# Interleaving two arrays on one core: 32 KiB store rows on two queues against 64 KiB store rows on one

## The chip, the cores and the metric

The kernel runs on one core of a Trainium2 chip. The metric is the device time of one execution in microseconds (us), given as the median of several runs. The work uses the core's 16 DMA engines, which move data between HBM (the chip's memory) and SBUF (the core's on-chip memory of 128 partitions), and VectorE (DVE), which copies within SBUF. SyncE (SP) and ScalarE (ACT) only issue DMAs here; each has a DMA queue of its own, and both queues feed the same 16 engines.

## The reference

Two float32 arrays of shape 32 x 256 x 1024 (8,388,608 elements, 33.5 MB each) are interleaved element by element into one of 32 x 256 x 2048 (67.1 MB):

```
result = np.zeros((batch, seq, dim * 2), dtype=np.float32)
result[..., 0::2] = x
result[..., 1::2] = y
```

Nothing is computed on the numbers. Since the interleave doesn't care where a row of 1024 ends, the arrays can be treated as flat: element i of x goes to 2i, element i of y to 2i + 1.

## The kernel before

The flat arrays are cut into 8 tiles of 128 partitions x 8192 elements (`WL`), 4 MiB of x and 4 MiB of y each. In a tile, partition p holds a contiguous run of 32 KiB of each input, and its output is a contiguous run of 64 KiB.

The loop over tiles (L44) loads x (L58) and y (L59) of a tile with one DMA each, on SP's queue; each moves one row of 32 KiB per partition. For the first tile, x is loaded in two halves, one on SP's queue and one on ACT's (L52 to L56). The pools `xpool` and `ypool` have two buffers each, so loads run up to two tiles ahead. After the first tile's loads, the "early" DMA (L64 to L67) writes 16 rows of 512 B from the y tile into the output region of the last tile, on ACT's queue, once y has landed. These bytes are overwritten by the last tile's own store; the write has no part in the result.

An inner loop (L70) takes the tile in two halves of 4096 columns (`WS`). For each half, DVE copies x into the even columns of an output buffer (L80) and y into the odd columns (L81), and ACT issues the store (L82): 128 rows of 32 KiB, each half of an output run. `opool` has two such output buffers of 32 KiB per partition. In SBUF the buffers take 64 + 64 + 64 = 192 KiB per partition.

The order of instructions on each engine is chosen by a scheduler from the program and its buffer dependencies; waits on semaphores are put in where a buffer is read or reused. Each transfer ends with one small packet per DMA engine that counts up the semaphore of that transfer.

After compiling, `tile_interleave_kernel` moves the first DMA of SP and of ACT ahead of the opening barrier (L97 to L115) and shortens the end (L120 to L129): GpSimd waits for the last transfers and clears the semaphores. The change does not touch this.

Of the kernel before, what the change touches and what calls it, by code (L numbers as in the profile page):

```python
# [3 lines left out]

# [4 lines left out]


@with_exitstack
def _interleave(
    ctx: ExitStack,
    tc: tile.TileContext,
    x: bass.AP,
    y: bass.AP,
    out: bass.AP,
):
    nc = tc.nc  # L20
    P = 128

    total = 1
    for s in x.shape:
        total *= s

    WL = 8192
    WS = 4096

    xf = x.rearrange("b s d -> (b s d)")  # L30
    yf = y.rearrange("b s d -> (b s d)")
    of = out.rearrange("b s d -> (b s d)")

    fp32 = mybir.dt.float32

    xpool = ctx.enter_context(tc.tile_pool(name="xp", bufs=2))
    ypool = ctx.enter_context(tc.tile_pool(name="yp", bufs=2))
    opool = ctx.enter_context(tc.tile_pool(name="op", bufs=2))

    lwidths = [WL] * (total // P // WL)  # L40
    assert sum(lwidths) == total // P

    start = 0
    for lw in lwidths:  # L44
        xtile = xpool.tile([P, WL], fp32, name="xtile")[:, :lw]
        ytile = ypool.tile([P, WL], fp32, name="ytile")[:, :lw]

        xs = dataclasses.replace(xf, offset=start, ap=[[lw, P], [1, lw]])
        ys = dataclasses.replace(yf, offset=start, ap=[[lw, P], [1, lw]])
        if start == 0:  # L50

            for q, c in ((nc.sync, 0), (nc.scalar, lw // 2)):  # L52
                q.dma_start(
                    out=xtile[:, c : c + lw // 2],
                    in_=dataclasses.replace(xf, offset=c, ap=[[lw, P], [1, lw // 2]]),
                )  # L56
        else:
            nc.sync.dma_start(out=xtile, in_=xs)  # L58
        nc.sync.dma_start(out=ytile, in_=ys)  # L59

        if start == 0:


            early = dataclasses.replace(  # L64
                of, offset=2 * (total - P * WL), ap=[[2 * WL, 16], [1, 128]]
            )
            nc.scalar.dma_start(out=early, in_=ytile[:16, :128])  # L67

        soff = 0
        while soff < lw:  # L70
            width = min(WS, lw - soff)
            otile = opool.tile([P, 2 * WS], fp32, name="otile")[:, : 2 * width]
            os_ = dataclasses.replace(
                of,
                offset=2 * start + 2 * soff,
                ap=[[2 * lw, P], [1, 2 * width]],
            )
            xsub = xtile[:, soff : soff + width]
            ysub = ytile[:, soff : soff + width]
            nc.vector.tensor_copy(out=otile[:, 0::2], in_=xsub)  # L80
            nc.vector.tensor_copy(out=otile[:, 1::2], in_=ysub)  # L81
            nc.scalar.dma_start(out=os_, in_=otile)  # L82
            soff += width

        start += P * lw
    assert start == total


def kernel(tc, x, y, out):
    nc = tc.nc  # L90
    _interleave(tc, x, y, out)
    tc.close()
    tc.compile()  # L93


    blocks = nc.main_func.blocks
    for engine in (mybir.EngineType.SP, mybir.EngineType.Activation):  # L97
        opening = blocks[0].instructions
        at, moved = next(
            (b, i)  # L100
            for b in blocks[1:]
            for i in b.instructions
            if i.engine == engine and i.opcode == "DMACopy"
        )
        assert not moved.sync_info.on_wait
        body = at.instructions
        body.remove(moved)
        gate = next(
            n
            for n, i in enumerate(opening)  # L110
            if i.engine == engine and i.opcode == "Drain"
        )
        opening.insert(gate, moved)
        at.instructions = body
        blocks[0].instructions = opening  # L115

    last = nc.main_func.blocks[-1]  # L120
    tail = last.instructions
    wait = tail[0]
    clear = next(n for n, i in enumerate(tail) if i.opcode == "ISA")
    assert wait.engine == mybir.EngineType.SP and wait.opcode == "Drain"
    assert wait.sync_info.on_wait and not wait.sync_info.on_update
    assert tail[clear].engine == mybir.EngineType.Pool
    last.instructions = [
        copy.replace(wait, engine=mybir.EngineType.Pool)
    ] + tail[clear:]  # L129


# [1 line left out]
_INS = ['x', 'y']  # L133
_OUTS = [((32, 256, 2048), 'float32')]


# [23 lines left out]
```

## Time and profile before

| what | value |
|---|---|
| median of 5 runs | 315.53 us (315.35 to 315.86) |
| the profiled execution | 315.58 us |
| its span, from the first to the last instruction | 313.8 us |
| bytes read from and written to HBM | 67.11 and 67.12 MB |
| mean rate over the span | 428 GB/s |
| DVE busy | 72.6 us (23%), 32 copies |
| L80, x copies 128 x 4096, each | 2295 ns |
| L81, y copies 128 x 4096, each | 2292 ns |
| DMA packets in all | 4784, of these 544 under 512 B |

How to read it: a DMA is cut into packets, one per row, spread evenly over the 16 engines; a packet has a start and a duration in the trace. The page's rows on queues give packets, MB, and the time that the packets took as a share of 16 engines' span. "q1" is SP's queue, "q10" ACT's. In an answer of the windows view, each row gives the stretch, its length, busy time and number of instructions of DVE and POOL, the granted TensorE clock, the DMA share and the GB/s moved. DMA shares above 1 come from counting a packet where it starts.

### The profile page before, as it was taken

To read this page: it belongs to the slowest core of one execution; us is meant where nothing else is said; L and a number is where in the kernel's file an instruction comes from. 1 tells how busy PE (TensorE), PEld (TensorE's weight loads), DVE (VectorE), ACT (ScalarE), POOL (GpSimd) and SP (SyncE) were. 2 spreads that over 40 slices of the span, in tenths; PEclk is the share of its full clock that TensorE was granted. 3 is DMA by queue.
4 is the path that set the end of the run, shared out by engine and by line. 5 is a ranking of instruction groups with operands and counts; after the bars stand their busy time and mean duration, and the time that the engine had idled before them with its cause. 6 is when DMAs were issued, how large, how long until landed. Compare 5 with 4: busy or idle time off the path is not lost.

```text
span 313.8 us, 139 instructions
## 1 busy us (share of the span) xinstructions
DVE 72.6 (23%) x32; POOL 0.2 (0%) x4
## 2 busy tenths in 40 slices
DVE  0523002231022410325003150131501305023500
POOL 0000000000000000000000000000000000000000
DMA  8999999999999999999999999999999999999997
GB/s 343 460 409 394 455 414 455 414 455 414 455 414 451 418 439 430 430 439 418 451 414 455 409 460 405 464 401 468 401 464 405 460 409 455 414 455 414 455 414 334
DMA packets 4784, 134.23 MB, mean 428 GB/s; under 512 B 544, under 2 KB 560, under 8 KB 560
## 3 DMA queue, kind: packets, MB, share of 16 engines
q10 hardware_dynamic: 2480, 69.22, 51.1%
q1 hardware_dynamic: 2304, 65.01, 48.4%
HBM read 67.11 MB, written 67.12 MB: 428 GB/s over the span
## 4 chain that ended last, share of the span: by engine, by line
DMA 83%; DVE 11%; DVEq 1%; issue 0%
DMA out_dram<-otile 76%; DMA ytile<-in_y_dram 7%; DVE otile L81 6%; DVE otile L80 5%; DVEq L93 1%; DVEq L80 0%
## 5 line engine op out<-in xcount | busy, mean ns | idle before, releaser
L80 DVE COPY otile<-xtile 128x4096 f32<-128x4096 f32 x16 | 36.6, 2295 | 185.8 <-DMA out_dram<-otile 174.1
L81 DVE COPY otile<-ytile 128x4096 f32<-128x4096 f32 x16 | 36.6, 2292 | 40.0 <-DMA ytile<-in_y_dram 40.0
L144 POOL MEMSET const-bfloat16-1.0<- 128x1 bf16 x1 | 0.1, 103 | 0.0
L144 POOL MEMSET const-uint8-127<- 128x1 uint8 x1 | 0.1, 103 | 0.0
L144 POOL MEMSET const-float32-1.0<- 128x1 f32 x1 | 0.1, 100 | 0.0
L144 POOL MEMSET const-float32-0.0<- 128x1 f32 x1 | 0.1, 99 | 0.2 <-issue 0.2
## 6 DMA issues: line engine op xcount, KB each, us to landing
out_dram<-otile ACTq DMA_DIRECT2D x16, 4096.0 KB, 29.1
ytile<-in_y_dram SPq DMA_DIRECT2D x8, 4096.0 KB, 60.8
xtile<-in_x_dram SPq DMA_DIRECT2D x7, 4096.0 KB, 43.6
xtile<-in_x_dram SPq DMA_DIRECT2D x1, 2048.0 KB, 11.7
xtile<-in_x_dram ACTq DMA_DIRECT2D x1, 2048.0 KB, 13.4
out_dram<-ytile ACTq DMA_DIRECT2D x1, 8.0 KB, 6.1
```

The costliest lines, as they stand in the source:

```text
L80: nc.vector.tensor_copy(out=otile[:, 0::2], in_=xsub)
L81: nc.vector.tensor_copy(out=otile[:, 1::2], in_=ysub)
L93: tc.compile()
L144: nc = _bacc.Bacc("TRN2", target_bir_lowering=False, num_devices=1)
```

## The change

The tile size stays at 128 x 8192. What changes is how a tile is stored and in which order DMAs are issued:

- the two half-tile output buffers become one buffer of 64 KiB per partition (`opool`, one buffer); a store moves 128 rows of 64 KiB, one per tile
- x and y of a tile share one buffer, `pair`, of 64 KiB per partition (x on the left, y on the right), two of them; SBUF use remains 192 KiB
- a weave is two copies of 8192 columns instead of four of 4096
- the last tile is woven not into the output buffer but into the `pair` buffer that tile 6 has left
- all stores and loads are on SP's queue, but for the second half of the first x, which stays on ACT's
- the order is the program's (`manual_schedule`): load 0, load 1, weave and store 0, load 2, weave and store 1, and so on to load 7, weave and store 6, weave and store 7
- the early small write is gone

```diff
-    WL = 8192
-    WS = 4096
+    W = 8192
+    n = total // (P * W)
+    assert n * P * W == total
...
-    xpool = ctx.enter_context(tc.tile_pool(name="xp", bufs=2))
-    ypool = ctx.enter_context(tc.tile_pool(name="yp", bufs=2))
-    opool = ctx.enter_context(tc.tile_pool(name="op", bufs=2))
+    inpool = ctx.enter_context(tc.tile_pool(name="inp", bufs=2))
+    opool = ctx.enter_context(tc.tile_pool(name="op", bufs=1))
+    ctx.enter_context(tc.manual_schedule())
...
+    def rows(flat, k, width):
+        return dataclasses.replace(
+            flat, offset=k * P * width, ap=[[width, P], [1, width]]
+        )
...
-        if start == 0:
-
-            for q, c in ((nc.sync, 0), (nc.scalar, lw // 2)):
+    def load(k):
+        pair = inpool.tile([P, 2 * W], fp32, name="pair")
+        if k == 0:
+            for q, c in ((nc.sync, 0), (nc.scalar, W // 2)):
                 q.dma_start(
-                    out=xtile[:, c : c + lw // 2],
-                    in_=dataclasses.replace(xf, offset=c, ap=[[lw, P], [1, lw // 2]]),
+                    out=pair[:, c : c + W // 2],
+                    in_=dataclasses.replace(xf, offset=c, ap=[[W, P], [1, W // 2]]),
                 )
         else:
-            nc.sync.dma_start(out=xtile, in_=xs)
-        nc.sync.dma_start(out=ytile, in_=ys)
+            nc.sync.dma_start(out=pair[:, :W], in_=rows(xf, k, W))
+        nc.sync.dma_start(out=pair[:, W:], in_=rows(yf, k, W))
+        return pair
 
-        if start == 0:
-
-
-            early = dataclasses.replace(
-                of, offset=2 * (total - P * WL), ap=[[2 * WL, 16], [1, 128]]
-            )
-            nc.scalar.dma_start(out=early, in_=ytile[:16, :128])
+    def weave(pair, woven):
+        for s in (0, 1):
+            nc.vector.tensor_copy(out=woven[:, s::2], in_=pair[:, s * W : (s + 1) * W])
 
-        soff = 0
-        while soff < lw:
...
-            nc.vector.tensor_copy(out=otile[:, 0::2], in_=xsub)
-            nc.vector.tensor_copy(out=otile[:, 1::2], in_=ysub)
-            nc.scalar.dma_start(out=os_, in_=otile)
-            soff += width
...
+    pairs = {0: load(0)}
+    for k in range(n):
+        if k + 1 < n:
+            pairs[k + 1] = load(k + 1)
+            woven = opool.tile([P, 2 * W], fp32, name="woven")
+        else:
+            woven = inpool.tile([P, 2 * W], fp32, name="pair")
+        weave(pairs.pop(k), woven)
+        nc.sync.dma_start(out=rows(of, k, 2 * W), in_=woven)
```

More of the change, by code (lines that the diff above doesn't have):

```diff
@@ L34, in _interleave @@
     fp32 = mybir.dt.float32
-    xpool = ctx.enter_context(tc.tile_pool(name="xp", bufs=2))
-    ypool = ctx.enter_context(tc.tile_pool(name="yp", bufs=2))
-    opool = ctx.enter_context(tc.tile_pool(name="op", bufs=2))
[L40 to L49, printed above, removed]
-        if start == 0:
-            for q, c in ((nc.sync, 0), (nc.scalar, lw // 2)):
+    inpool = ctx.enter_context(tc.tile_pool(name="inp", bufs=2))
@@ L59, in _interleave @@
-        nc.sync.dma_start(out=ytile, in_=ys)
-        if start == 0:
-            early = dataclasses.replace(
-                of, offset=2 * (total - P * WL), ap=[[2 * WL, 16], [1, 128]]
-            )
-            nc.scalar.dma_start(out=early, in_=ytile[:16, :128])
-        soff = 0
-        while soff < lw:
[L71 to L79, printed above, removed]
-            nc.vector.tensor_copy(out=otile[:, 0::2], in_=xsub)
-            nc.vector.tensor_copy(out=otile[:, 1::2], in_=ysub)
-            nc.scalar.dma_start(out=os_, in_=otile)
-            soff += width
@@ L85, in _interleave @@
-        start += P * lw
-    assert start == total
+                    out=pair[:, c : c + W // 2],
+                    in_=dataclasses.replace(xf, offset=c, ap=[[W, P], [1, W // 2]]),
+                )
+        else:
+            nc.sync.dma_start(out=pair[:, :W], in_=rows(xf, k, W))
[4 more added lines that the diff above has]
+            nc.vector.tensor_copy(out=woven[:, s::2], in_=pair[:, s * W : (s + 1) * W])
```

## The prediction

> **What bounds the kernel now.** I read the page first, then the windows view over the whole span, then the DMA view of two short windows, then the packet records of the trace themselves (start, duration, size and queue of each DMA packet), because the views do not resolve what this change turns on.
>
> ```profile
> span 313.8 us, 139 instructions
> ...
> DVE 72.6 (23%) x32; POOL 0.2 (0%) x4
> ...
> q10 hardware_dynamic: 2480, 69.22, 51.1%
> q1 hardware_dynamic: 2304, 65.01, 48.4%
> ...
> DMA 83%; DVE 11%; DVEq 1%; issue 0%
> ```
>
> Queue 10 is the ACT queue (stores, half of the first x), queue 1 the SP queue (loads). Their packets together fill 51.1 + 48.4 = 99.5% of 16 engines' span. The chain says DMA 83%, DVE 11%, which looks as if 11% could be won from the copies; the queue rows say no: while a copy is on the chain the engines are still moving the other queue's bytes. So the bound is the number of bytes times the pace of an engine, and the only time to win or lose is time in which an engine moves nothing. The windows show where that is:
>
> ```profile
> 0.00:3.10 3.10, 0.00 (x0) 0.20 (x4) 1.00 0.74 233
> 3.10:25.80 22.70, 8.28 (x4) 0.00 (x0) 1.00 1.00 430
> 25.80:29.60 3.80, 0.71 (x1) 0.00 (x0) 1.00 1.14 407
> 29.60:285.00 255.40, 56.83 (x25) 0.00 (x0) 1.00 1.00 433
> ```
>
> The last two columns are the DMA share and GB/s. All is flat at 430 to 433 GB/s but for two places: the first 3 us (233), and 25.8 to 29.6 us (407 although the engines are "1.14" busy: packets that take longer than their bytes need). The second place is where the kernel writes to HBM for the first time. Is one queue alone enough to fill the engines, and is one direction alone as fast as both mixed? Two windows of the DMA view answer, 14 to 25 us (loads only) and 290 to 312 us (stores only):
>
> ```profile
> q1 hardware_dynamic: 164, 4.85, 102.1%
> ```
>
> ```profile
> q10 hardware_dynamic: 320, 9.44, 99.3%
> ```
>
> Yes, in both. Mixing costs nothing either: in the packet records the start-to-start distance on one engine is 1209.3 to 1209.45 ns (means of the four pairs) for a 32 KiB packet from 29.6 us to the end, whichever of load and store it is and whichever comes next.
>
> **The change, step by step, for one of the 16 engines** (the work is split evenly, so one engine's sum is the span's).
>
> 1. *Longer store rows.* Start-to-start distances in the packet records: 23.4 ns for 512 B, 607.06 for 16 KiB, 1209.45 for 32 KiB. From the last two, 16 KiB more cost 602.39 ns, so a packet has 607.06 - 602.39 = 4.7 ns that do not depend on its size; 512 B gives 23.4 - 18.8 = 4.6, the same. A 64 KiB packet is not in the trace; the line through three sizes gives 2 x 1204.78 + 4.7 = 2414.3 ns. Bounds: nothing saved if a row is still moved as two packets (2418.9), 4.7 saved if it is one. A loss is not excluded by a row, but three sizes on one line speak against it. I take one packet: 64 packets less per engine x 4.7 = 0.30 us.
> 2. *Fewer transfers.* Each transfer ends with a 4-byte semaphore packet per engine; the next packet starts 6 ns after it. Before: 17 loads, 16 stores and the early write make 34 (the 544 "under 512 B" of the page are 34 x 16). After: 17 + 8 = 25. 9 x 6 ns = 0.05 us. The early write's data (L67, 8 KB in all) goes too: 23 ns on its engine. Together 0.08 us.
> 3. *All stores on SP's queue.* A store now stands in SP's program behind the wait for its weave, and the next pair's two loads stand behind it. That hurts only if the ring runs dry meanwhile. A pair load of 8 MiB takes 16 x 1209 + 12 ns = 19.4 us, a store 19.3 us. While SP waits for weave k, load k+1 is still running in the ring. One copy of 4096 columns takes 2.29 us and two in a row 4.50 us from start to end, so a weave of two 8192-column copies is 8.8 to 9.1 us. Issues of 0.33 to 0.52 us on SP are hidden the same way.
> 4. *One output buffer.* Weave k+1 must wait until store k has landed. From then: 0.4 us (last store packet to the waiting instruction, 312.81 to 313.21 us) + 9.1 us weave + about 1 us until a fresh issue moves data (0.00 to 0.99 us at the start) = 10.5 us, beside load k+2, 19.4 us long and issued before it. Cover left: 8.9 us per tile, so the cost is nothing; without that cover it would be about 10.5 us for each of 7 tiles.
>    The Trainium skill ("Trainium Kernel Development and Optimization", section Best Practices) says to double-buffer so that DMA and compute overlap, which speaks against this step. By that rule the single buffer would expose the weaves; the rows above say another transfer is in the ring each time.
> 5. *The last tile* goes into the pair buffer that weave 6 has freed. Its weave needs load 7 and weave 6, not store 6, so it runs in the first 9.1 us of store 6 (19.3 us), and store 7 is queued some 10 us before it is needed. The end remains an engine's last packet plus 0.94 us (312.81 to 313.75).
> 6. *Start.* The first x halves, y and the second pair are issued in the same order on the same queues: nothing changes up to 26 us.
> 7. *No early small write.* This is the unknown. Between 25.86 and 27.70 us, 27 load packets take 1.23 to 1.97 us instead of 1213 ns. Their excess sums to 0.73 us per engine. It starts right behind the 512 B packets, and comes back behind the early write's semaphore packets; the first 32 KiB stores at 29.07 us already run at 1213 ns. Two readings: the first write to HBM costs this whoever makes it (then store 0 pays it at about 41 us), or it belongs to the small write and to the switch between queues (then it goes). The nearest row is the other first: the first loads of the kernel take 1088 to 1554 ns for 16 KiB instead of 611, and 0.62 us per engine are lost there. Two firsts, two similar prices: I take "it stays, 0.73". Ends: 0 and, for a first packet of 64 KiB that has nothing to hide behind, twice that (1.46).
>
> **Sum:** 0.30 + 0.08 = 0.385 us less per engine, nothing added. The profiled execution took 315.58 us (span 313.8, 1.8 around it); 315.58 - 0.385 = 315.20. The median of the runs is 0.05 lower (315.53), so the forecast is 315.15 us, 0.12% less than before. About 0.2% (0.63 us) is what a measurement of this kernel can tell from no change (its five runs span 0.16%).
>
> **Rivals.**
> - *The stall of 0.73 us goes with the small write.* For: the loss ends before the first large store, which pays nothing itself. Against: it could be that store's entrance fee, paid early. Then 315.53 - 0.385 - 0.73 = 314.4.
> - *The first write costs more when it is a whole tile's first row*, at most the double: 315.15 + 0.73 = 315.9, still within the bound.
> - *The long row is still two packets*: 0.30 is not saved, 315.45. The change then does nothing that can be seen.
> - *Slower: each turn of the one ring costs.* Before, an engine never goes longer than 3.1 us without a load or without a store packet once stores have begun. After, it loads for 19.4 us, then stores for 19.3, in one ring. After the first write there are 6 more returns to writing and 6 to loading. If a return to writing costs what the first did, 6 x 0.73 = 4.4 us: 319.5. It decides early: the verdict is slower from 0.63 + 0.385 = 1.0 us in all, that is 0.17 us per return to writing, or 0.085 us per turn of either kind. Against it: turns between packets of the two queues, some 3,000 of them, cost nothing; and store-to-store and load-to-load borders within one queue cost 6 ns. What is not in the trace is a turn within a ring, or after a long pause.
>
> The Trainium skill prices a return differently ("HBM Reference", section Latency): 0.2 us on average for an access, 2 us under high load. If 12 turns each cost 0.2 us, the time would be 2.4 us longer; no run here shows such a wait at a turn.
>
> **Chances.** Stall stays: 0.42. Stall gone: 0.32. Stall larger: 0.07. Row still two packets: 0.03. Turns cost: 0.16. So faster by over 0.2% 0.32, within 0.2% 0.52, slower 0.16. The range takes in the gone stall (314.4, and 0.2 for the scatter of runs) and, above, the doubled stall and the mild end of the turns (0.1 us each, 315.15 + 1.2): 314.2 to 316.5. What lies outside is the dear end of the turns. The likeliest case by itself is 314.9 to 315.5.
>
> **What would show it.** In the changed kernel's page: queue 1 near 99% with all but the first half-x, 1024 store packets of 64 KiB and 400 packets under 512 B; DMA digits without a dip. In the packet records: 2414 ns between starts of store packets (step 1); no gap ahead of a store or load (steps 3 to 5), with DVE idle ahead of each weave waiting for the store before; around 41 us load or store packets with an excess, summing to 0.73 us per engine or to none (step 7). The forecast is wrong if packets lengthen at every turn, or if the ring is dry when a store is issued.

## The result and the profile after

The changed kernel takes 317.05 us in the median of 23 runs (315.61 to 318.18); the kernel before, on the same chips, 315.57 us in 44 runs (315.31 to 316.83). The ratio is 1.0037 with an interval of 1.0027 to 1.0047: **slower by 0.4%**, where 0.1% faster was forecast. What stands out is the scatter: 2.6 us between its runs, a few tenths between most runs of the kernel before.

The profiled execution of the changed kernel is its fastest run (315.61 us) and looks like the forecast. Its page:

```profile
span 313.8 us, 88 instructions
...
DVE 70.3 (22%) x16; POOL 0.2 (0%) x4
...
q1 hardware_dynamic: 3456, 132.12, 97.9%
q10 hardware_dynamic: 144, 2.10, 1.6%
...
DMA 71%; DVE 17%; SPq 0%; issue 0%; DVEq 0%
```

One queue carries nearly everything and fills the engines (97.9 + 1.6 = 99.5%, as before with two). 400 small packets and 1024 store packets of 64 KiB are there, and the mean distance from one store packet's start to the next on an engine is 2414.4 ns (forecast 2414.3). The order on SP's and DVE's side is as reckoned, in the timeline (start, duration, engine, line, operation, and idle time ahead with what ended it):

```profile
61.93 8.77 DVE L61 COPY woven<-pair 128x8192 f32<-128x8192 f32 x2 [35.49 <-DMA out_dram<-woven]
70.73 0.34 SPq L71 DMA_DIRECT2D out_dram<-woven  x1
71.17 0.38 SPq L55 DMA_DIRECT2D pair<-in_x_dram  x1
71.59 0.43 SPq L56 DMA_DIRECT2D pair<-in_y_dram  x1
100.63 8.77 DVE L61 COPY woven<-pair 128x8192 f32<-128x8192 f32 x2 [29.93 <-DMA out_dram<-woven]
```

Each weave waits for the store before it (35.49 and 29.93 us of idle DVE) and its own store is issued at 70.73 us, about 8 us before load 2 is through (79 us). The ring, that is what a queue still holds for an engine to move, never runs dry. Windows of the same execution:

```profile
3.10:36.00 32.90, 8.86 (x2) 0.00 (x0) 1.00 1.02 441
36.00:41.20 5.20, 0.00 (x0) 0.00 (x0) 1.00 0.89 315
41.20:60.00 18.80, 0.00 (x0) 0.00 (x0) 1.00 1.03 446
62.00:78.00 16.00, 8.70 (x2) 0.00 (x0) 1.00 1.03 444
```

The stretch from 36 to 41 us, ahead of the first store, is where the loss of the first write now stands (315 GB/s; packets counted where they start make the neighbours look high): 0.85 us per engine, against 0.73 before. So this profile doesn't show why the median is 317.05.

**Where the time is when it takes longer.** The changed kernel was run once more and caught at 318.07 us. The trace doesn't name a packet's engine, but on one engine a packet starts 3 to 4 ns before the last one ends, so packets can be strung into 16 chains. "Excess" below is a packet's duration over 611 ns (16 KiB), 1213 (32 KiB) or 2418 (64 KiB), what such packets take undisturbed. The sum over all engines is no larger than in the 315.61 us execution (1.75 us per engine, 1.79 there). But 15 engines end between 312.0 and 312.9 us and one at 315.4. In the windows view, the end of the execution of 315.61 us, then the end of the repeated one of 318.07 us:

```profile
312.90:315.40 2.50, 0.00 (x0) 0.00 (x0) 1.00 0.00 0
```

```profile
312.90:315.40 2.50, 0.00 (x0) 0.00 (x0) 1.00 0.06 26
```

A share of 0.06 and 26 GB/s is one engine of sixteen at its full pace, alone for 2.5 us. How it came to be late, at the seven changes from loads to stores ("turns"), from the chains:

```
turn at us         39    78.9   117.5   156   195   234   273
late by, us       0.83   0.96    1.86   3.01  3.01  3.10  3.39
its excess, ns     876    474     654    866     0   378     0
others, each  352-1260  0-108    0-56  0-168  0-21  0-16  0-39
```

"Late by" is the start of its last load packet after that of the first engine, "excess" that of its last two load packets ahead of the stores. "Late by" already holds what the last load but one lost: the 866 ns at 156 us are part of the 3.01 us in the same column. At the first turn everybody pays; over the six later ones the late engine loses 2.37 us, each other one 0.01 to 0.17 us, and what it loses it is later by from then on.

### The profile page after: what moved, and what is told of

Same layout as the page of the kernel before. It is cut to its first block, busy times and chain, and to the rows that moved or that the text cites. A ratio compares the mean times of both kernels' runs of the same rounds, so it can differ in the third digit from the quotient of the medians.

```text
span 313.8 us, 88 instructions
## 1 busy us (share of the span) xinstructions
DVE 70.3 (22%) x16; POOL 0.2 (0%) x4
## 3 DMA queue, kind: packets, MB, share of 16 engines
q1 hardware_dynamic: 3456, 132.12, 97.9%
## 4 chain that ended last, share of the span: by engine, by line
DMA 71%; DVE 17%; SPq 0%; issue 0%; DVEq 0%
DMA out_dram<-woven 49%; DMA pair<-in_y_dram 22%; DVE woven L61 15%; DVE pair L61 1%; SPq L55 0%; SPq L71 0%; DVEq L61 0%
## 5 line engine op out<-in xcount | busy, mean ns | idle before, releaser
L61 DVE COPY woven<-pair 128x8192 f32<-128x8192 f32 x14 | 61.4, 4426 | 202.9 <-DMA out_dram<-woven 185.3
L61 DVE COPY pair<-pair 128x8192 f32<-128x8192 f32 x2 | 8.9, 4428 | 5.9 <-DMA pair<-in_y_dram 5.2
```

What stands on the lines that cost most here:

```text
L61: nc.vector.tensor_copy(out=woven[:, s::2], in_=pair[:, s * W : (s + 1) * W])
```

## The experiments

The edits are against the changed kernel unless said otherwise. Each figure is a median with the range of its runs.

**1. The changed kernel again** (no edit).

> The changed kernel again, nothing edited, to see an execution that is slower than the profiled one. The profiled execution took 315.61 us and lost only some 0.2 us per engine in late load packets (1214 to 1221 ns instead of 1213), while the median is 317.05. Theory 'reading alone' (all 16 engines read HBM at once, with no store packets between, and then a read is now and then late): in an execution of 317 us or more the excess of load packets over 1213 ns sums to about 1.5 us per engine, spread over the load stretches; store packets stay at 2418 ns. Rival 'turns': the excess stands in the last load packet ahead of a store or the first packet behind it, some 0.2 us at each of 12 turns. Rival 'first write': it stands at 36 to 41 us, 2.3 us instead of 0.85. Median expected between 316.3 and 317.5 by all three.

Measured: 317.89 us (317.43 to 318.07), the trace above. None of the three expectations describes it. The loss does stand at the turns, but on one engine, not on all. Late loads within the load stretches (1214 to 1221 ns) amount to some 0.1 us per engine, so "reading alone" isn't it; the first write costs 0.75 us, so it isn't that either. From here on I took up "the late reader".

**2. The early small write put back.**

```diff
+        if k == 0:
+            early = dataclasses.replace(
+                of, offset=2 * (total - P * W), ap=[[2 * W, 16], [1, 128]]
+            )
+            nc.scalar.dma_start(out=early, in_=pair[:16, W : W + 128])
```

> The changed kernel with the early small write put back (16 rows of 512 B on ACT's queue when the first y has landed; the last tile's store overwrites it). 'First write': the loss at 36 to 41 us moves to about 26 us and shrinks to 0.73 us per engine, and the median falls to that of the kernel before, about 315.5 us, with a scatter of a few tenths. 'Reading alone' and 'turns': the stall moves, but the median stays at 316.5 to 317.3 us with a scatter of 2 us.

Measured: 317.73 us (316.36 to 318.29). The 512 B packets ran at 26.0 to 26.5 us, and in the windows view nothing happened there:

```profile
24.00:36.00 12.00, 2.51 (x1) 0.00 (x0) 1.00 1.00 429
36.00:41.20 5.20, 0.00 (x0) 0.00 (x0) 1.00 0.91 328
```

The loss stays ahead of the first large store (0.79 us per engine). "First write" as the cause of the median falls. In the same profile the two engines that end last, 2.3 and 1.5 us behind the median engine, lost 2.18 and 1.66 us at the six later turns, the others 0.03 to 0.61 us: the late reader again.

**3. Stores cut into two of 32 KiB rows.**

```diff
-        nc.sync.dma_start(out=rows(of, k, 2 * W), in_=woven)
+        for h in (0, 1):
+            nc.sync.dma_start(
+                out=dataclasses.replace(
+                    of, offset=2 * k * P * W + h * W, ap=[[2 * W, P], [1, W]]
+                ),
+                in_=woven[:, h * W : (h + 1) * W],
+            )
```

> The changed kernel with each store cut in two of 32 KiB rows, as the kernel before stores them (halves of a tile), both on SP's queue; the rest as changed. By the sum of the prediction this costs 64 more data packets x 4.7 ns + 8 semaphore packets x 6 ns = 0.35 us: about 317.4 us. If long rows are themselves the trouble, the median falls to about 315.6 us. 'Reading alone', 'turns' and 'first write' all expect no fall: 317.0 to 317.5 us.

Measured: 318.12 us (317.25 to 318.46), beside 317.89 for the repeat on the same chip. A difference of 0.2 is in line with the 0.35 of the sum, and lies within the scatter. Long rows aren't the trouble. Here too the two engines that end last lost most at the six later turns, 2.98 and 1.98 us, the others 0.03 to 1.17 us.

**4. Tiles of 4096 columns, twice the turns.**

```diff
-    W = 8192
+    W = 4096
```

> The changed kernel with tiles of 4096 columns instead of 8192: 16 tiles, twice as many turns in the ring (28 after the first write instead of 12), each stretch of loads or stores half as long (9.7 us); store rows are 32 KiB. Packets and semaphores cost 0.3 + 0.2 us more by the sum. 'Turns': the 1.5 us that the median lies above the kernel before doubles, 318.5 to 319.5 us. 'Reading alone': the engines read alone for as long in all, so the loss stays, 317.0 to 317.7 us, or falls if a stretch has to last a while before reads get late. 'First write': 317.0 to 317.7 us.

Measured: 323.29 us (322.75 to 324.0). More than "turns" expected: the packets' excess is 5.1 us per engine (1.79 in the 315.61 us execution), it falls on many engines, and the last engine ends 3.4 us behind the median one. From 30 us on, 0.9 us per engine stand in the last four loads ahead of a store, 2.0 in the last store ahead of a load and 0.6 in the first load behind it. The turns are the place, here in both directions; their price is not a constant.

**5. and 6. One engine made late, first try**, in both kernels: 17 rows of the first y loaded again, on ACT's queue.

```diff
+        if k == 0:
+            nc.scalar.dma_start(
+                out=pair[:17, W : W + 512],
+                in_=dataclasses.replace(yf, offset=0, ap=[[W, 17], [1, 512]]),
+            )
```

> The changed kernel, with 17 rows of 2 KiB of the first y loaded a second time on ACT's queue. 17 has no divisor up to 16 but 1, so one engine should get all 17 packets, 17 x 80 ns = 1.4 us more, at about 26 us, and be late from then on; the others get nothing. Theory 'the late reader' (at a turn from loads to stores, the engine that is still on its last loads while the others have begun to write is held up, and is later still at the next turn): this engine pays 0.1 to 0.9 us at most of the six later turns, as the late one did in the repeated run (0.96 us late at the second turn, 3.4 us at the last), and ends 3 to 5 us behind the others: 317.8 to 320 us, and every run is slow, with few near 316. Rival 'a turn costs any engine by chance': the late engine ends 1.4 us late plus what chance gives, 317.5 to 318.5 us, and the excess falls on other engines as often.

> The control: the same 17 extra packets on one engine in the kernel before, whose loads and stores take turns packet by packet out of two queues. The extra load also holds one engine's first pass back by 1.4 us. 'The late reader': there is no stretch in which all others write, so lateness isn't added to; the engine ends 0.9 to 1.4 us after the others and the time is 316.4 to 317.0 us. If lateness costs here too, over 317.5 us.

Measured: 325.17 (324.91 to 325.37) and 320.77 us (319.1 to 321.21). The first tells nothing of the question. The 17 packets took turns with 32 KiB loads of the other queue, one each 1.29 us, and landed at 42 us. The weave of the changed kernel waited for them:

```profile
42.62 4.43 DVE L66 COPY woven<-pair 128x8192 f32<-128x8192 f32 x1 [24.68 <-DMA pair<-in_y_dram]
```

The ring ran dry at 41 us. The extra load has to go where nobody waits for it (experiments 9 and 10). In the kernel before (profile of the 321.21 us run) the rings are dry for only 0.25 us per engine; after 42 us some 210 loads are held up, all along the span, 2.7 us per engine and on every engine. So a kernel on two queues can lose time this way too.

**7. Each store waits until the next pair has landed**, so that no load is left at a turn to stores.

```diff
...
+        if k + 1 < n:
+            nxt = pairs[k + 1]
+            for c in (W - 1, 2 * W - 1):
+                nc.vector.tensor_copy(out=spare, in_=nxt[:, c : c + 1])
+            nc.vector.tensor_copy(
+                out=woven[:, 2 * W - 2 : 2 * W - 1], in_=pair[:, W - 1 : W]
+            )
         nc.sync.dma_start(out=rows(of, k, 2 * W), in_=woven)
```

> The changed kernel, where each store (but the last) is issued only when the next pair has landed: after a weave DVE copies one column of each half of the next pair to a spare column and writes one column of the output again, so nobody reads HBM while others write at a turn from loads to stores. The ring is empty for some 1.7 us at each of 7 such turns (0.4 us landing, 0.3 us of small copies, 1.0 us until an issue moves data): some 12 us more than 315.2, so 326 to 329 us. 'The late reader': no load packet at the later turns is over by more than 30 ns, lateness stays below 1 us, and the runs scatter by a few tenths instead of 2 us. 'A turn costs in itself': the excess stays, now in the first store packets, with the scatter.

Measured: 333.79 us (333.75 to 333.88). Half of the expectation holds: no load packet ahead of a store is held up, and the scatter is gone (0.13 us). But the time is 5 us over. The windows view around two gaps ahead of stores and two returns to loads:

```profile
40.50:42.50 2.00, 0.22 (x2) 0.00 (x0) 1.00 0.00 0
56.00:62.50 6.50, 0.00 (x0) 0.00 (x0) 1.00 0.86 323
82.00:84.10 2.10, 0.22 (x2) 0.00 (x0) 1.00 0.45 187
97.00:104.00 7.00, 0.00 (x0) 0.00 (x0) 1.00 0.80 300
```

The gaps of 1.7 to 2.1 us are as meant. At each of the 6 returns to loads, though, all engines lose 0.82 to 0.88 us, in the last store packet and the first loads, where the changed kernel loses nothing. 315.2 + 7 x 1.9 + 6 x 0.83 = 333.5. The 0.73 us of the first write, which 315.2 holds, is not lost here, while each of the 7 first stores behind a gap loses 0.08 us; with that it is 333.3, half a us short of the measured time. Behind a gap, all 16 engines start within 0.15 us of each other.

**8. The kernel before without its early small write** (the block at L61 to L67 taken out).

> The kernel before without its early small write, nothing else. In the changed kernel with the early write, the 512 B packets at 26 us cost 27 ns each and no load near them was late; the loss stood in the two loads ahead of the first large store. So here the loss should stay at 0.7 us per engine, in the loads ahead of the first store, and the time should be within 0.2 us of the kernel before (315.4 to 315.7). If the small write itself paid, or paid in place of something dearer, the time moves by 0.5 us or more.

Measured: 315.49 us (315.28 to 315.73), ratio 0.9995 (0.9987 to 1.0004). As expected; the loss ahead of the first store is 0.67 us per engine.

**9. One engine made late, with a load that nobody waits for.**

```diff
...
             pairs[k + 1] = load(k + 1)
+            if k == 0:
+                nc.sync.dma_start(
+                    out=spare,
+                    in_=dataclasses.replace(yf, offset=0, ap=[[W, 17], [1, 512]]),
+                )
```

> The changed kernel with 17 rows of 2 KiB of y loaded into a spare tile that nobody reads, on SP's queue behind load 1. All 17 packets go to one engine (the earlier try showed that), 17 x 80 ns = 1.4 us, so one engine comes 0.8 to 1.4 us late to the first turn, and nothing else waits. Theory 'the late reader' (at a turn from loads to stores the engine still loading while others have begun to write is held up): that engine loses 0.1 to 0.9 us at most of the six later turns; it ends 2 to 5 us behind the others; median 317.8 to 320, no run under 316.8. Rival 'chance falls on any engine': 1.0 to 1.4 us on top of 315.2, and the usual scatter of 0 to 2.5 us on whichever engine: 316.4 to 318.

Measured: 318.81 us, **every run between 318.67 and 318.97**. One chain holds all 17 extra packets, 1.4 us; on top of them it loses 0.68 us at the second turn, 0.12 and 0.33 us at two of the five later ones, and ends at 315.9 us; 14 others end by 312.8, one at 313.7 (it lost 1.1 us at later turns with no extra packet). In this profile the engine made late is held up at later turns. The times alone say less: the rival's own terms, 315.2 + 1.4 and 0 to 2.5 us of scatter, reach up to 319.1, and the unedited kernel's six runs of experiment 1 scattered by no more than 0.6 us. Experiment 15 is the stronger test. That 17 rows land on one engine is what the Trainium skill ("DMA: Bandwidth & Descriptors", section Why a DMA increments its semaphore by 16 and not by 1) states: as many engines as the largest divisor up to 16; the trace agrees.

**10. The same in the kernel before** (spare load behind the second pair).

> The control: the same spare load in the kernel before, on SP's queue behind the second pair. 'The late reader', if it needs a stretch in which all others write: the engine ends 0.9 to 1.4 us behind the others and the time is 316.4 to 317.0 us with a scatter of a few tenths. If lateness is punished here too, where every engine changes from load to store with each packet: 318 us or more.

Measured: 322.53 us (319.04 to 325.07). The forecast for the control is wrong: the kernel before suffers from the extra load too, and more. But the profile (of the 319.04 us run) shows another path than held-up loads. After 42 us packets lose 0.25 us per engine in all. The small packets took turns with stores, so that one engine ends its last load at 290.8 us, the others between 282.2 and 283.9; the last copy of y, which began at 287.77 us in the kernel before, waits for it:

```profile
292.35 2.30 DVE L90 COPY otile<-ytile 128x4096 f32<-128x4096 f32 x1 [5.89 <-DMA ytile<-in_y_dram]
```

Meanwhile 15 engines have nothing to move for 2.0 to 2.5 us from 293 us on:

```profile
292.00:294.50 2.50, 2.15 (x1) 0.00 (x0) 1.00 0.37 157
```

So this run speaks neither for the late reader nor against it. The slower runs of this kernel, up to 325.07 us, have no profile.

**11. Two tiles per turn**: three buffers in rotation, the order load, load, store, store.

```diff
-    inpool = ctx.enter_context(tc.tile_pool(name="inp", bufs=2))
-    opool = ctx.enter_context(tc.tile_pool(name="op", bufs=1))
+    inpool = ctx.enter_context(tc.tile_pool(name="inp", bufs=3))
...
+    pairs = {}
+    for g in range(0, n, 2):
+        for k in (g, g + 1):
+            pairs[k] = load(k)
+        for k in (g, g + 1):
+            woven = inpool.tile([P, 2 * W], fp32, name="pair")
+            weave(pairs.pop(k), woven)
+            nc.sync.dma_start(out=rows(of, k, 2 * W), in_=woven)
```

> The changed kernel with half as many turns: three 64 KiB buffers in rotation, and on SP's queue load, load, store, store (two tiles) in place of load, store. Same packets, same bytes; 4 turns from loads to stores instead of 7, of which the first has its own loss of 0.7 to 0.85 us. No dry ring is expected (each weave has some 9 us of other transfers beside it). 'Turns, paid by late engines': what lies above 315.2 us (2.1 us in the median of all runs) falls to about half, 316.0 to 316.6 us. Rival 'reading alone': loads take as long in all without stores beside them, so no fall: 317.0 to 317.8 us.

Measured: 315.84 us (315.57 to 316.84), ratio to the kernel before 1.0005 (0.9994 to 1.0015). Same bytes, same packets, the same one queue and long rows, 4 turns to stores instead of 7: the loss is gone nearly whole, a little more than expected. 11 of its 12 runs lie under 316 us, 5 of 23 of the changed kernel; that one was not run unedited on this chip, but experiment 9 shows an engine late without help there. In its trace, of the 315.65 us run, no engine's last two loads lose more than 34 ns at the three later turns, and no engine is alone at the end. It is no faster than the kernel before either.

**12. The stores on ACT's queue**, the rest as changed.

```diff
-        nc.sync.dma_start(out=rows(of, k, 2 * W), in_=woven)
+        nc.scalar.dma_start(out=rows(of, k, 2 * W), in_=woven)
```

> The changed kernel with its stores on ACT's queue instead of SP's, nothing else: the one queue undone, the long rows and the single output buffer kept. A store and the pair load that is issued with it now alternate packet by packet and end together, so there is nothing in the rings while the next weave (8.8 us + 1.7 us of landing, issue and start) runs: 6 x 10.5 us = 63 us more, about 378 us. That is the cover that the fixed order on one queue gives. 'The late reader': load packets in the mixed stretches are at 1213 ns, no engine comes late.

Measured: 348.4 us (three runs from 343.1 to 344.6, three from 352.2 to 352.9; the profile is of a run of 352.43). Wrong in both halves. Rings without work cost some 12.5 us (the span less the packets' time per engine is 14.0 us, in the kernel before 1.5), not 63, and packets got long: 26 us of excess per engine, where the kernel before has 1.35. How the two groups of runs differ isn't known. Windows early and late:

```profile
55.00:80.00 25.00, 8.76 (x2) 0.00 (x0) 1.00 0.99 425
...
120.00:160.00 40.00, 1.08 (x2) 0.00 (x0) 1.00 0.97 355
```

Until 117 us loads of 32 KiB and stores of 64 KiB take turns at full pace. From 121 us, after a gap of 1.9 to 3.5 us on 15 engines, they don't find it again until 300 us: engines 97% busy, 355 GB/s.

**13. to 16. Seven engines or all sixteen set back by 1.22 us**, in both kernels: the spare load with 49 or 112 rows of 1152 columns in place of 17 of 512.

> The kernel before with a spare load of 49 rows of 4.5 KiB on SP's queue behind the second pair (nobody reads it). 49 is 7 x 7, so 7 of the 16 engines get 7 packets each, 7 x 174 ns = 1.22 us, about one 32 KiB packet: from then on 7 engines would store while 9 load, and the other way round. Theory 'out of step' (a load is held up while other engines write; the kernel before is spared because its engines change between load and store together): loads lose time all along, 27 ns or more each as in the first late-engine run of this kernel, 320 us or more, with a scatter of over 1 us. Rival 'only a last one pays': 7 late engines are no loners, the time is 315.6 + 1.2 = 316.8 us.

> The control for it: 112 rows of the same size, 7 on each of the 16 engines, so that all are late by 1.22 us and stay in step. Both theories: 315.6 + 1.2 = 316.8 us, scatter of some 0.3 us, no load packet held up after 42 us. If it is the spare load itself that does harm, 318 us or more.

> The changed kernel with the 49 rows on 7 engines, behind load 1. 'Out of step': at each turn from loads to stores 7 engines still load for 1.2 us while 9 write; each loses 0.1 to 0.5 us per later turn, 6 turns: 317.5 to 320 us, every run over 317. 'Only a last one pays': 316.4 plus the usual 0 to 2.5 us.

> Its control: 112 rows, 7 on each engine of the changed kernel, all late by 1.22 us. Both theories: the changed kernel's own times plus 1.2 us, 316.8 to 319.3 us, with its scatter of 2 us, since nothing is changed in how the engines stand to each other.

Measured: kernel before, seven engines 319.37 us (318.71 to 324.06), all sixteen 317.09 (316.84 to 317.14); changed kernel, seven 317.94 (317.58 to 318.96), all 318.24 (317.91 to 319.43). In the kernel before, taking engines out of step costs 3.8 us, the set-back of all alone 1.5. But the profile (of the 318.71 us run) doesn't support "a load is held up while others write". From 66 to 280 us some 550 loads ran there beside 4 to 12 stores of other engines, all within 6 ns of 1213, and the rate of the long middle stretch is undiminished:

```profile
66.00:280.00 214.00, 49.94 (x22) 0.00 (x0) 1.00 1.00 433
```

It lost 1.1 us per engine once, between 58 and 65 us, in the stores of the seven engines beside their spare packets and then in the first large loads behind them, and hardly anything after.

The times of the pair for the changed kernel tell nothing apart, but the profile of the run with seven late engines (318.96 us) does. What each engine lost in its last two loads, at the first turn and summed over the six later ones:

```
                      first turn, us   six later turns, us
seven engines set back   0.65-1.21          0.56-1.36
nine others              0.55-1.06          0.01-0.04
```

Within one execution, the engines set back by hand pay at the later turns and the others don't; the spare load is through long before. With all sixteen set back (profile of the 318.28 us run) the loss falls on all of them, 0.05 to 1.59 us.

**17. The loads wait until the store has landed** (the gap at the other turn).

```diff
...
+            if last is not None:
+                nc.vector.tensor_copy(out=last[1][:, :1], in_=spare)
+                nc.vector.tensor_copy(out=last[0][:, :1], in_=last[1][:, :1])
             pairs[k + 1] = load(k + 1)
...
+        last = (pair, woven)
```

> The changed kernel with the ring run dry at the other turn: the next pair's loads are issued only when the store has landed (DVE then writes one column of the stored buffer and one of the freed pair buffer, both overwritten later), 6 times. After each such gap all 16 engines start their loads together, within 0.15 us, as they did behind the gaps of the run that waited for loads, and the next store is queued behind those loads. In that earlier run every engine lost 0.75 to 0.85 us at each turn that came after a common start, though none was late. Theory 'a new order costs' (16 engines that change direction in a standing order of starts lose nothing, engines out of that order, or all of them after a common start, lose up to 1 us until they stand in one again): some 0.7 us per engine at each turn from loads to stores, 7 times, in the last loads; 315.2 + 6 x 1.8 (gaps) + 6 x 0.7 = 330 us. Rival 'returning to loads is the dear turn': no load packet is held up but at the first store; 326 us.

Measured: 339.49 us (339.01 to 339.78). Windows around a gap, the next turn to stores, and the next gap:

```profile
59.00:63.50 4.50, 1.84 (x3) 0.00 (x0) 1.00 0.37 102
80.00:84.00 4.00, 0.00 (x0) 0.00 (x0) 1.00 1.00 328
101.00:106.50 5.50, 2.18 (x3) 0.00 (x0) 1.00 0.60 203
```

At 80 to 84 us nothing is dry (share 1.00), yet only 328 GB/s move: the engines lose 0.96 us each, at a turn that costs the changed kernel under 0.1 us in the mean of its engines. The loss comes at all 6 later turns to stores, 0.9 to 1.1 us, and 0.5 to 0.75 us more at each start of loads behind a gap. These starts are not common, as was expected: the engines begin 0.6 to 1.1 us apart, and in a new order. From one turn to the next the rank correlation of their starts (1 would be the same order) is 0.1 to 0.7 here, 0.92 or more in the 315.61 us execution of the changed kernel. "Returning to loads is the dear turn" expected none of it and falls; "a new order costs" has the place right and expected too little: the gaps measure 2.35 us in the mean, not 1.8, so 6 x 2.35 and 9.9 us of losses make 339.2 from 315.2, where the profiled run took 339.38.

## Why the prediction was wrong

**The bound and the sum** (steps 1 and 2) were right. A 64 KiB row is one packet at 2414.4 ns, 400 small packets remain, and the engines' undisturbed work shrank as worked out. (Two readings were a little off without effect: the first loads took from 787 ns, not 1088, and no load follows a load after 29.6 us, so there are three pairs, not four.) The fastest run confirms the whole: 315.58 - 0.385 + 0.44 (excess of 1.79 us per engine against 1.35) = 315.63, measured 315.61.

**The queue, the single buffer, the last tile** (steps 3 to 5) were right: each weave has another transfer beside it, the ring is never dry, and the engines end within 0.9 us in the profile of 315.61 us. The single output buffer cost nothing, so the rule of the Trainium skill that was weighed there (double-buffering, "Trainium Kernel Development and Optimization", Best Practices) asks for overlap, and the fixed order gave it.

**The early small write** (step 7): the value taken, "it stays", was right: 0.85 us per engine against 0.73. My reason for leaving a third of the chance to "it goes" was a misreading of the trace: the two late packets stood behind the small write because the first large store came two packets later. Experiments 2 and 8 show it: the small write costs nothing, and without it the loss stays.

**What failed is the zero for a turn within the ring**, the "nothing added" of the sum; step 3 asked only whether the ring runs dry. It was argued from some 3,000 changes between the two queues that cost nothing. Those turns are of another kind: all 16 engines of the kernel before change from load to store with the same packet, in an order of starts that stays the same within 1 ns from 36 to 180 us and within 0.1 us to the end. That this is why they cost nothing is not shown: with seven engines out of step they cost nothing either from 66 us on (13), while with one engine set back loads lost 2.7 us per engine (6). The rival "each turn of the one ring costs" had the place right (12 later turns, decisive from 0.085 us per turn; in the median (317.05 - 315.15) / 12 = 0.16 us came out) but the payer wrong: not each engine at each return, but the late one, whose lateness grows (2.37 us at six turns to stores in the 318.07 us execution, the others 0.01 to 0.17). It got 0.16 of the chance and the range ended below it. The prediction's 2.4 us for 12 turns of 0.2 us also comes near the measured time, by luck: it takes the latency of an access for the price of a turn, and in the 318.07 us execution 15 engines lost less than a tenth of it.

**Shown:** what the 318.07 us execution has over the 315.61 us one is one engine's (1); in other slow executions the engines that end last are those that lost most at the turns (2, 3); engines set back by hand pay at later turns while the others of the same execution don't (15); fewer turns take the loss away with the bytes, the packets and the queue kept (11), more turns raise it (4); behind a gap in which all rings are dry, all engines lose at the next turn, 0.8 to 1.1 us in the mean, in either direction (7, 17). **Ruled out** as the cause: the long rows (3), the missing small write (2, 8), loads without stores beside them (1, 11). **Open:** what in the chip holds the packets back. That engines need a standing order of starts, and lose time until they have one, fits 1, 7, 15 and 17, and is a description, not a mechanism; 4, where the loss is mostly at returns to loads without any gap, it doesn't explain. Which engine falls behind in an unedited run, and why, is open. Why a packet mix of 32 and 64 KiB doesn't settle again after 121 us (12), and what a late engine costs the kernel before (6, 10 and 13 show three different paths), isn't settled either.

## What to carry to other kernels

When the DMA engines are the bound, look at the slowest of the 16 engines, not at their mean: a busy share of 98.7% (97.1 + 1.6 in the 318.07 us execution) and an unchanged sum of packet times hid 2.5 us. A change of direction within one ring was not free here for an engine that was late, nor for any engine behind a dry ring; make few of them (two tiles per turn took the loss away) or let two queues alternate packet by packet, as the kernel before does, and keep odd-shaped small transfers, which fall on a few engines, out of both. And when a changed kernel scatters where the old one didn't, profile it again before explaining anything: the first profile was its fastest run.

## What the runs showed of the hardware that was not expected

- Seven engines set back by 1.22 us lost 0.56 to 1.36 us each at the six later turns from loads to stores, nine others 0.01 to 0.04 us (15).
- A load of 34 KB on one engine, 1.4 us of its work, costs the kernel before 7 us (322.53 against 315.68). In the profiled run (319.04 us) its packets took turns with stores, the engine's last load ended 7 us after the others', and 15 engines ran dry for 2.0 to 2.5 us.
- The loss ahead of a turn is seen in the packets before it: the first large store costs 0.63 to 0.98 us per engine in every kernel with loads in flight ahead of it, taken from the last one or two loads; a store that starts from a dry ring shows 0.08 us.
- A packet has 4.7 ns that do not depend on its size from 512 B to 64 KiB (23.4, 607.06, 1209.45 and 2414.4 ns from start to start).
- The copy of 128 x 8192 takes 4.43 us where two of half the width take 2.29 each.
